# First layer's attention: one inverse of the softmax sums and a row of four scalings per four heads

## The chip, the cores and the metric

One core of a Trainium2 chip runs the whole program. The metric is the device time of one execution in microseconds (us). TensorE (PE) does matmuls, VectorE (DVE) and ScalarE (ACT) work on tiles of 128 partitions, GpSimd (POOL) does a few elementwise steps, and SyncE (SP) issues most DMA transfers. Each engine takes its instructions strictly in the order in which they stand in its queue.

## The reference

The program is a two-layer diffusion trunk over 512 latent and 256 context tokens of width 1024. The first layer mixes tokens in two ways at once: 8 heads of attention, and 8 heads of a linear recurrence that runs in both directions ("state mixing"). Their outputs are joined, multiplied by `w_out`, and an MLP follows. The part that the change touches is the softmax of the attention:

```python
s_lat = jnp.einsum('bqgrd,bkgd->bgrqk', q, kl) * scale      # latent keys
s_ctx = jnp.einsum('bqgrd,bkgd->bgrqk', q, kc) * scale      # context keys
p_lat, p_ctx = joint_softmax([s_lat, s_ctx])                # over both
o = einsum('bgrqk,bkgd->bqgrd', p_lat, vl) + einsum('bgrqk,bkgd->bqgrd', p_ctx, vc)
```

Context queries read the 256 context tokens only; latent queries read all 768 tokens.

## The kernel before

Attention and state mixing of the first layer share one stage. Tokens are cut into six tiles of 128; tiles 0 and 1 are context, 2 to 5 latent.

**Attention.** `attend` (lines 1126 to 1160) takes one tile of queries. Its 8 heads come as two groups of four (`g`), and a group shares keys and values. For each head `j` of a group: matmuls write the scores into `ps` (tag `sc`, two banks of PSUM, one buffer), DVE takes the row maximum (L1149) and makes the bias (L1151), ACT computes the exponentials into a tile `prob` with the row sum as a by-product (L1154), DVE inverts the sum (L1155), and ACT scales `prob` by it (L1156). `prob` has five buffers, so the second score of a group needs a buffer that the group before has to give back. Then `weighted` (lines 323 to 345) goes over the tiles of keys: four transposes (L332) put a 128x128 piece of each head into a bank `pt` (two buffers), ACT or DVE in turn copies it to `pts` (L337, L335), and a matmul adds values times weights to `po` (L341). Two such matmuls for neighbouring tiles use different halves of the array. At its end, ACT copies half of `po` and DVE adds the other half into `oa` (L344, L345), which ACT's queue stores to `oD` in DRAM (L1160). A group of a latent tile has 4 scores, 24 transposes, 6 copies and 6 value products; one of a context tile 4, 8, 2 and 2, on 256 keys.

**State mixing.** A chain of 24 steps. In a step: matmul `x` from the state (L1026), DVE add `xs`, matmul `u` (L1036), DVE `vu` (L1041, twice), matmul `s` (L1051), DVE `state` (L1059). Around the chain stand the preparation of the next block (`z`, `xv`, L985 to L1005) and the outputs (`y`, L1070 to L1080). When a pair of token tiles is complete, `finish` normalizes it: mean and variance on DVE and ACT, transposes `yt` (L1116), products `oy` (L1120, L1123), and a store to `oD` by POOL's queue (L1124). Loads `gg` for it stand in SP's queue (L1087, L1088) and wait for a buffer that L1123 gives back.

**What sets the order.** All functions are generators. The loop `state_mixing` moves them along: attention first gets 40 steps, then 5 per step of the chain, 120 in all. A step of the generator ends at each `yield`, so the place of a `yield` decides when its instructions are written down, and with that their priority; a scheduler then sorts each engine's queue by priority and by when it thinks the inputs are there. The chain has high priority, attention fills in. At the stage's end comes the product with `w_out` (L1302) for three segments: context (tiles 0, 1), the middle latent tiles (3, 4) and the outer ones (2, 5). It loads `raw` from `oD` (L1293), splits it into a high and a low part (`xr`, or `dh` and `dl`; L279 on ACT, L280 on DVE), and multiplies by weights which are split in the same way (`wraw`, `whi`, `wlo`). Its first PSUM bank is the one of the scores. One output tile of 256 columns takes 24 matmuls, and each segment has 8 such tiles.

Of the kernel before, what the change touches and what calls it, by code (L numbers as in the profile page):

```python
# [10 lines left out]
F32 = mybir.dt.float32  # L11
F32R = mybir.dt.float32r
AF = mybir.ActivationFunctionType
ALU = mybir.AluOpType
AX = mybir.AxisListType
# [3 lines left out]
P = 128  # L19
# [205 lines left out]
def tile_trunk(ctx: ExitStack, tc: tile.TileContext, t: dict, out, cc: Cols, pc: Cols):  # L225
    nc = tc.nc
    V, A, G, T = nc.vector, nc.scalar, nc.gpsimd, nc.tensor
# [7 lines left out]
    def u(s):  # L235
        uid[0] += 1
        return f"{s}_{uid[0]}"
# [648 lines left out]
    with ExitStack() as sb:  # L886
        psum_pool(sb, zy=(2, 1), ch=(1, 1), po=(1, 1), pt=(2, 1), sc=(1, 2))
        tp = pool("attention", stack=sb, side="right")
# [238 lines left out]
        def attend(qi, keys):  # L1127
# [9 lines left out]
            V.tensor_tensor(out=qs[64:128], in0=qr[64:128], in1=qs[64:128].bitcast(F32), op=ALU.subtract)  # L1137
            o = tp.tile([P, 512], F32, tag="oa", name=u("oa"), bufs=1)
            for g in (0, 1):
                prob = []  # L1140
                for j in range(4):
                    ps = psum("sc", "sc")
                    for s in SEGS:
                        if s[0] >= P * kt1:
                            continue
                        for m, kx in enumerate((kh, kl)):
                            T.matmul(ps[:, cols2(s)], lhsT=qs[:, 2 * j + g, :], rhs=kx[:, g, s[0]:s[0] + s[1]], start=m == 0, stop=m == 1)  # L1147
                    st = tp.tile([P, 4], F32, tag="st", name=u("st"), bufs=6)
                    V.tensor_reduce(out=st[:, 0:1], in_=ps[:, c0:c1], op=ALU.max, axis=AX.X)  # L1149
                    sc = sq8[:, qi, 2 * j + g:2 * j + g + 1]  # L1150
                    V.tensor_scalar(out=st[:, 1:2], in0=st[:, 0:1], scalar1=sc, scalar2=-1.0, op0=ALU.mult, op1=ALU.mult)  # L1151
                    pr = tp.tile([P, NT], F32, tag="prob", name=u("prob"), bufs=5)
                    pv = pr[:, 0:c1 - c0]
                    A.activation(out=pv, in_=ps[:, c0:c1], func=AF.Exp, scale=sc, bias=st[:, 1:2], accum_out=st[:, 2:3])  # L1154
                    V.reciprocal(out=st[:, 3:4], in_=st[:, 2:3])  # L1155
                    A.activation(out=pv, in_=pv, func=AF.Copy, scale=st[:, 3:4])  # L1156
                    prob.append(pr)
                    yield
                yield from weighted(prob, vtok, g, list(range(kt0, kt1)), o, tp)
            nc.scalar.dma_start(oD[0:4, :, P * qi:P * qi + P].rearrange("a q c -> q a c"), o.rearrange("p (a c) -> p a c", c=P))  # L1160

# [104 lines left out]
    with ExitStack() as sc:  # L1266
# [8 lines left out]
        scale = norm_scale(0, 4, "nmlp")  # L1275
# [528 lines left out]
```

## Time and profile before

| | us |
|---|---|
| median of 3 runs | 2008.81 (2007.28 to 2010.16) |
| the profiled execution: its own time | 2009.51 |
| its span, first to last instruction | 2007.7 |
| first `s` of the chain starts | 366.22 |
| last `s` of the chain starts | 612.20 |
| PE busy over the span | 1896.6 (94%) |
| DVE, ACT busy | 1215.2 (61%), 840.7 (42%) |

A busy PE is a modelled figure, because matmuls overlap: in a dense stretch, the distance from one start to the next says more than a duration. Times in the trace are counted from the first instruction.

### The profile page before, as it was taken

What the parts mean: (1) busy time and instruction counts of PE and PEld (TensorE: products, weight loads), DVE (VectorE), ACT (ScalarE), POOL (GpSimd) and SP (SyncE); (2) the same over time, 40 slices, a digit from 0 to 9 for tenths busy, and PEclk for the clock granted to TensorE, in tenths of its full rate; (3) what the DMA queues carried; (4) which work ended last, traced back from release to release, by engine and by line L of the source; (5) the groups of instructions that cost most, each with busy time, mean ns of one, the idle gap of its engine ahead of it and who ended that gap; (6) DMA issues with size and microseconds to landing.
All of it is one profiled execution on the core that took longest, in us unless ns stands there. A gap on an engine that the chain in (4) does not pass through costs nothing.

```text
span 2007.7 us, 34218 instructions
## 1 busy us (share of the span) xinstructions
PE 1896.6 (94%) x13992; PEld 1545.1 (77%) x13992; DVE 1215.2 (61%) x2150; ACT 840.7 (42%) x1419; POOL 294.2 (15%) x291
## 2 busy tenths in 40 slices
PE   6999988899998999999999999899899789999997
PEld 4776756776765998888888889778578488888886
DVE  5567979775677765654544444865687464444445
ACT  3344442555544552232223224544566454333335
POOL 0000014432321520000000002310153120000001
PEclk9999998899998999999999999999999799999998
DMA  9355575742414733344444422212101133333333
GB/s 336 121 166 171 182 228 148 156 89 56 98 44 132 251 107 99 122 124 136 125 125 121 136 84 80 76 53 74 32 1 53 32 95 105 95 92 97 95 97 113
DMA packets 147884, 228.18 MB, mean 114 GB/s; under 512 B 65024, under 2 KB 102288, under 8 KB 147600
## 3 DMA queue, kind: packets, MB, share of 16 engines
q1 hardware_dynamic: 140912, 213.54, 36.1%
q10 hardware_dynamic: 5456, 7.73, 1.1%
q0 software_dynamic: 1360, 4.73, 0.7%
q8 instruction: 110, 1.80, 0.4%
q14 instruction: 46, 0.38, 0.1%
HBM read 200.00 MB, written 25.96 MB: 113 GB/s over the span
## 4 chain that ended last, share of the span: by engine, by line
PE 77%; DVE 9%; DMA 7%; ACT 3%; issue 3%; POOL 1%; SPq 0%; DVEq 0%; POOLq 0%; ACTq 0%
PE m L367 37%; PE win L367 13%; PE po L341 4%; DMA wmod<-in_wmod_dram 4%; PE pt L332 3%; PE z L985 2%; DVE wlo L280 2%; PE sc L1147 2%; PE wout L1718 1%; PE wout L1302 1%; PE s L1051 1%; PE mod L405 1%; PE lora L653 1%; PE z L1560 1%; DVE junk L1319 1%
## 5 line engine op out<-in xcount | busy, mean ns | idle before, releaser
L279 ACT ACTIVATE whi<-wraw 128x1024 fp32r<-128x1024 f32 x214 | 226.4, 1059 | 678.0 <-PE m L367 561.0
L280 DVE TENSOR_TENSOR wlo<-wraw,whi 128x1024 fp32r<-128x1024 f32 x214 | 264.4, 1236 | 212.2 <-ACT whi L279 209.4
L367 PE MATMUL m<-hh,whi 128*128 128x512 f32 (+1 forms) x816 | 239.3, 344 | 4.9 <-ACT relu L1241 2.4
L367 PE MATMUL m<-hl,whi 128*128 128x512 f32 (+1 forms) x816 | 241.2, 343 | 0.2 <-POOL hl L503 0.2
L367 PE MATMUL m<-hh,wlo 128*128 128x512 f32 (+1 forms) x816 | 241.3, 344 | 0.0
L367 PE MATMUL m<-dl,whi 128*128 128x256 f32 (+1 forms) x832 | 240.7, 341 | 0.0
L367 PE MATMUL m<-dh,whi 128*128 128x256 f32 (+1 forms) x832 | 238.6, 342 | 1.7 <-DVE xl L1223 1.6
L367 PE MATMUL m<-dh,wlo 128*128 128x256 f32 (+1 forms) x832 | 239.8, 341 | 0.1
L367 PEld LDWEIGHTS m<-dh,whi 128*128 128x128 f32 x832 | 153.3, 188 | 23.9 <-DVE xl L1223 4.9
L367 PEld LDWEIGHTS m<-hh,whi 128*128 128x128 f32 x816 | 152.1, 188 | 24.7 <-ACT relu L1241 2.8
L471 POOL TENSOR_TENSOR acc<-acc,nsq 128x256 f32<-128x256 f32 x42 | 42.8, 1027 | 865.8 <-ACT nsq L470 861.0
L367 PEld LDWEIGHTS m<-hl,whi 128*128 128x128 f32 x816 | 153.6, 188 | 19.4 <-POOL hl L503 0.4
L367 PEld LDWEIGHTS m<-dl,whi 128*128 128x128 f32 x832 | 153.8, 188 | 19.0
L367 PEld LDWEIGHTS m<-dh,wlo 128*128 128x128 f32 x832 | 153.7, 188 | 18.9 <-DVE wlo L280 0.3
L367 PEld LDWEIGHTS m<-hh,wlo 128*128 128x128 f32 x816 | 153.4, 188 | 19.0 <-DVE wlo L280 0.3
L367 PE MATMUL win<-hl,whi 128*128 128x512 f32 (+1 forms) x512 | 162.3, 348 | 4.7 <-POOL hl L503 3.5
L367 PE MATMUL win<-hh,whi 128*128 128x512 f32 (+1 forms) x512 | 162.3, 362 | 2.7 <-ACT hh L498 2.7
L367 PE MATMUL win<-hh,wlo 128*128 128x512 f32 (+1 forms) x512 | 160.2, 345 | 0.0
L1319 DVE SCALAR_TENSOR_TENSOR junk<-wmod,crow 128x1024 f32<-128x1024 f32 x64 | 78.5, 1226 | 118.5 <-DMA wmod<-in_wmod_dram 117.9
L1223 DVE SCALAR_TENSOR_TENSOR xl<-m,modT,xl 128x512 f32<-128x512 f32 (+1 forms) x144 | 97.4, 686 | 72.3 <-PE m L367 72.3
L367 PEld LDWEIGHTS win<-hh,whi 128*128 128x128 f32 x512 | 95.4, 194 | 33.6 <-issue 15.7
L367 PEld LDWEIGHTS win<-hl,whi 128*128 128x128 f32 x512 | 98.5, 193 | 22.9 <-issue 5.7
(413 smaller groups left out, 3560.0 us busy)
## 6 DMA issues: line engine op xcount, KB each, us to landing
wraw<-in_w_dram SPq DMA_DIRECT2D x136, 512.0 KB, 3.6
wmod<-in_wmod_dram SPq DMA_DIRECT2D x96, 512.0 KB, 4.2
wraw<-in_wout_dram SPq DMA_DIRECT2D x40, 512.0 KB, 3.7
wraw<-in_win_dram SPq DMA_DIRECT2D x35, 512.0 KB, 4.4
arD<-ar SPq DMA_DIRECT2D x8, 768.0 KB, 4.5
kbD<-kb SPq DMA_DIRECT2D x8, 768.0 KB, 6.5
ari<-arD SPq DMA_DIRECT2D x24, 256.0 KB, 3.9
kbd<-kbD SPq DMA_DIRECT2D x48, 128.0 KB, 3.9
```

Source lines behind the costliest of these rows:

```text
L279: A.activation(out=hi, in_=src, func=AF.Copy)
L280: (lo_eng or V).tensor_tensor(out=lo, in0=src, in1=hi.bitcast(F32), op=ALU.subtract)
L332: T.transpose(pt[:, P * j:P * j + P], prob[j][:, P * m:P * m + P], ident)
L341: T.matmul(po[HALVES[i], :], lhsT=vt[:, k_, r], rhs=w_, start=m_ < 2, stop=m_ + 2 >= n, tile_position=(0, 64 * i))
L367: T.matmul(part(ps, s), lhsT=a[:, c], rhs=row(b, k, s), start=first and j == 0 and q == 0, stop=last and j == n - 1 and q == 2)
L405: T.matmul(ps[r:r + 32, :], lhsT=cs[:, k, :], rhs=wm[:, c], start=k == 0, stop=k == KT - 1, tile_position=(0, r))
L471: (V if k == KT - 1 else eng).tensor_tensor(out=at(acc, s), in0=at(acc, s), in1=at(sq, s), op=ALU.add)
L653: T.matmul(ps[s][d][:, 0:s[1]], lhsT=LORA[wname][r, P * p:P * p + P], rhs=src[r, tokens(s)], start=True, stop=True, tile_position=(64 * d, 0))
L985: T.matmul(ps[:, P * (2 * a + c):P * (2 * a + c) + P], lhsT=kb[:, 2 * m + a, c, :], rhs=ar[:, 2 * m + a, c, :], start=True, stop=True)
L1147: T.matmul(ps[:, cols2(s)], lhsT=qs[:, 2 * j + g, :], rhs=kx[:, g, s[0]:s[0] + s[1]], start=m == 0, stop=m == 1)
L1223: V.scalar_tensor_tensor(out=xs, in0=part(ps, s), scalar=mod(l, which, m, s[2]), in1=xs, op0=ALU.mult, op1=ALU.add)
L1319: V.scalar_tensor_tensor(out=junk, in0=wm, scalar=1.0, in1=crow[:, :, v], op0=ALU.mult, op1=ALU.mult, accum_out=modT[:, l, n, v:v + 1])
```

## The change

Per group of four heads, the four small tiles `st` (128x4, six buffers) become one tile of 128x4x4 (three buffers): a row of maxima, one of biases, one of sums and one of inverses. The loop over heads now ends with the exponentials. After it stand two more steps of the generator: an empty one, then one with a single `reciprocal` of four columns and the four scalings one after the other.

```diff
             for g in (0, 1):
-                prob = []
+                prob, st = [], tp.tile([P, 4, 4], F32, tag="st", name=u("st"), bufs=3)
                 for j in range(4):
                     ps = psum("sc", "sc")
...
-                    st = tp.tile([P, 4], F32, tag="st", name=u("st"), bufs=6)
-                    V.tensor_reduce(out=st[:, 0:1], in_=ps[:, c0:c1], op=ALU.max, axis=AX.X)
+                    V.tensor_reduce(out=st[:, 0, j:j + 1], in_=ps[:, c0:c1], op=ALU.max, axis=AX.X)
...
-                    A.activation(out=pv, in_=ps[:, c0:c1], func=AF.Exp, scale=sc, bias=st[:, 1:2], accum_out=st[:, 2:3])
-                    V.reciprocal(out=st[:, 3:4], in_=st[:, 2:3])
-                    A.activation(out=pv, in_=pv, func=AF.Copy, scale=st[:, 3:4])
+                    A.activation(out=pr[:, 0:c1 - c0], in_=ps[:, c0:c1], func=AF.Exp, scale=sc, bias=st[:, 1, j:j + 1], accum_out=st[:, 2, j:j + 1])
                     prob.append(pr)
                     yield
+                yield
+                V.reciprocal(out=st[:, 3], in_=st[:, 2])
+                for j in range(4):
+                    A.activation(out=prob[j][:, 0:c1 - c0], in_=prob[j][:, 0:c1 - c0], func=AF.Copy, scale=st[:, 3, j:j + 1])
+                yield
                 yield from weighted(prob, vtok, g, list(range(kt0, kt1)), o, tp)
```

Two more `yield`s in each of 12 groups make 128 steps of attention where there were 104. The 40 steps ahead of the chain and the 5 per step of it are as before. So the scheduler's order changes on every engine from the first step of the chain on. Counted in PE's queue ahead of the last `s` of the chain: of 48 scores 46 before, now 43; of 224 transposes 192, now 176; of 56 value products 46 (22 alone, 12 times two neighbours together), now 44 (18 alone, 13 times two). Behind it stand 2 scores, 32 transposes and 10 value products (all alone) before; now 5 scores, 48 transposes and 12 value products (10 alone, one pair). Up to the first `s` of the chain, PE's queue is the same.

The first place is PE's queue at the end of the stage, where the scores of the last group (`sc`) stand just ahead of the first product with `w_out` (`wout`). Before, the last rows ahead of it are these, with one score:

```order
L1070 MATMUL y_7041<-state_6986,ard_3282 64x64
L1072 MATMUL y_7041<-vu_7037,z_3286 64x64
L1072 MATMUL y_7041<-vu_7039,z_3287 64x64
L1116 MATMUL yt_7072<-cst,yacc 128x128 x4
L1147 MATMUL sc_5701<-kh,qs_5245 128x256
L1147 MATMUL sc_5701<-kl,qs_5245 128x256
L1147 MATMUL sc_5701<-kh,qs_5245 128x512
L1147 MATMUL sc_5701<-kl,qs_5245 128x512
L332 MATMUL pt_5725<-cst,prob_5688 128x128
L332 MATMUL pt_5743<-cst,prob_5688 128x128
L1302 MATMUL wout_7184<-xr,whi_7180 128x256 x2
```

Now two scores stand there, behind the value products of the group before:

```order
L341 MATMUL po_5869<-pts_5957,vtok 64x512
L1148 MATMUL sc_6091<-kh,qs_5642 128x256
L1148 MATMUL sc_6091<-kl,qs_5642 128x256
L1148 MATMUL sc_6091<-kh,qs_5642 128x512
L1148 MATMUL sc_6091<-kl,qs_5642 128x512
L341 MATMUL po_5869<-pts_6027,vtok 64x512
L1148 MATMUL sc_6111<-kh,qs_5642 128x256
L1148 MATMUL sc_6111<-kl,qs_5642 128x256
L1148 MATMUL sc_6111<-kh,qs_5642 128x512
L1148 MATMUL sc_6111<-kl,qs_5642 128x512
L1116 MATMUL yt_7027<-cst,yacc 128x128 x4
L1116 MATMUL yt_7038<-cst,yacc 128x128 x4
```

The first `wout` follows on the last row. From the last `s` of the chain to this point, PE's queue now holds five scores and all six value products of the group before, where it held two scores and four value products. Behind the first 24 `wout` matmuls, 24 transposes and 6 value products of the last group follow in both; before, they stood together, now 24 further `wout` matmuls stand among them.

The second place is DVE's queue between the bias of the last group's third score (`st_6052<-st_6052,sq_99`, L1151) and the split of the context rows (`xr`, L280), which the first `wout` reads. Before, from the maximum of the last score on:

```order
L1149 TENSOR_REDUCE st_5706<-sc_5701 128x1
L280 TENSOR_TENSOR wlo_7214<-wraw_7211,whi_7213 128x1024
L1123 TENSOR_TENSOR oy_7077<-oy_7077,gg_6472 128x512
L1100 TENSOR_SCALAR mean_7082<-mean_7082 128x8 x2
L1151 TENSOR_SCALAR st_5706<-st_5706,sq_99 128x1
L1101 TENSOR_TENSOR yacc<-yacc,mean_7082 128x512 x2
L1155 RECIPROCAL st_5706<-st_5706 128x1
L280 TENSOR_TENSOR xr<-raw_7165,xr 128x4x256 x2
```

Now:

```order
L1151 TENSOR_SCALAR st_6052<-st_6052,sq_99 128x1
L280 TENSOR_TENSOR dl_7097<-raw_7094,dh_7096 128x4x256
L1111 TENSOR_TENSOR yacc<-yacc,var_7011 128x512 x2
L1149 TENSOR_REDUCE st_6052<-sc_6111 128x1
L280 TENSOR_TENSOR wlo_7142<-wraw_7139,whi_7141 128x1024
L1120 TENSOR_TENSOR oy_7032<-yt_7027,gg_6857 128x256 x2
L1151 TENSOR_SCALAR st_6052<-st_6052,sq_99 128x1
L1120 TENSOR_TENSOR oy_7043<-yt_7038,gg_6860 128x256 x2
L1123 TENSOR_TENSOR oy_7032<-oy_7032,gg_6857 128x512
L1123 TENSOR_TENSOR oy_7043<-oy_7043,gg_6860 128x512
L1157 RECIPROCAL st_6052<-st_6052 128x4
L280 TENSOR_TENSOR xr<-raw_7093,xr 128x4x256 x2
```

Both splits of the middle tiles (`dl_7097`) and the end of `finish` for the last two tiles now stand ahead of the split of the context rows. ACT's queue has the same order: the exponentials of the last two scores, then `xr`, then the four scalings.

The third place is ACT's queue during the first `w_out` tiles, from the weights of the third tile (`whi_7176`) to those of the sixth (`whi_7281`); `dh_7098` is the outer segment, and its second row reads the attention rows that `L1162 DMA oD` stores:

```order
L279 ACTIVATE whi_7176<-wraw_7174 128x1024
L337 ACTIVATE pts_6228<-pt_6223 128x512
L467 ACTIVATE acc<-xc 128x256
L337 ACTIVATE pts_6264<-pt_6259 128x512
L279 ACTIVATE dh_7098<-raw 128x4x256
L337 ACTIVATE pts_6352<-pt_6347 128x512
L279 ACTIVATE whi_7211<-wraw_7209 128x1024
L344 ACTIVATE oa_5645<-po_6222 64x512
L1162 DMA oD<-oa_5645 128x4x128
L279 ACTIVATE whi_7246<-wraw_7244 128x1024
L279 ACTIVATE dh_7098<-raw 128x4x256
L279 ACTIVATE whi_7281<-wraw_7279 128x1024
```

Before, both rows of the outer segment stood together, one weight tile later: behind the weights of the sixth tile, ahead of those of the seventh. DVE's queue mirrors this with `dl_7099` ahead of `wlo_7282`.

More of the change, by code (lines that the diff above doesn't have):

```diff
@@ L1147, in attend @@
                             T.matmul(ps[:, cols2(s)], lhsT=qs[:, 2 * j + g, :], rhs=kx[:, g, s[0]:s[0] + s[1]], start=m == 0, stop=m == 1)
-                    st = tp.tile([P, 4], F32, tag="st", name=u("st"), bufs=6)
-                    V.tensor_reduce(out=st[:, 0:1], in_=ps[:, c0:c1], op=ALU.max, axis=AX.X)
+                    V.tensor_reduce(out=st[:, 0, j:j + 1], in_=ps[:, c0:c1], op=ALU.max, axis=AX.X)
                     sc = sq8[:, qi, 2 * j + g:2 * j + g + 1]
-                    V.tensor_scalar(out=st[:, 1:2], in0=st[:, 0:1], scalar1=sc, scalar2=-1.0, op0=ALU.mult, op1=ALU.mult)
+                    V.tensor_scalar(out=st[:, 1, j:j + 1], in0=st[:, 0, j:j + 1], scalar1=sc, scalar2=-1.0, op0=ALU.mult, op1=ALU.mult)
                     pr = tp.tile([P, NT], F32, tag="prob", name=u("prob"), bufs=5)
[L1153 to L1156, printed above, removed]
+                    A.activation(out=pr[:, 0:c1 - c0], in_=ps[:, c0:c1], func=AF.Exp, scale=sc, bias=st[:, 1, j:j + 1], accum_out=st[:, 2, j:j + 1])
                     prob.append(pr)
                     yield
+                yield
[3 more added lines that the diff above has]
+                yield
                 yield from weighted(prob, vtok, g, list(range(kt0, kt1)), o, tp)
```

## The prediction

> **What bounds the kernel now.** I read the page's chain first, then a table by stages, then the waits in the stage that the change touches.
>
> ```profile
> PE 77%; DVE 9%; DMA 7%; ACT 3%; issue 3%; POOL 1%; SPq 0%; DVEq 0%; POOLq 0%; ACTq 0%
> 366.00:613.00 247.00, 241.78 (x3620) 179.72 (x3620) 172.75 (x401) 137.00 (x271) 74.50 (x66) 0.98 0.37 80
> 613.00:633.00 20.00, 13.22 (x157) 7.66 (x153) 14.03 (x31) 7.60 (x12) 2.47 (x3) 0.88 0.42 132
> 633.00:648.00 15.00, 14.32 (x62) 8.66 (x61) 11.56 (x18) 7.30 (x10) 2.93 (x1) 0.82 0.64 211
> 648.00:718.00 70.00, 67.89 (x564) 66.38 (x563) 55.81 (x84) 40.16 (x65) 39.69 (x36) 1.00 0.72 229
> ```
>
> The columns of the last four are the stretch, its length, busy time (and instructions) of PE, PE's weight loads, DVE, ACT and POOL, the granted TensorE clock, the DMA share, and GB/s. The chain of the state runs from 366 to 613, and PE is idle there for 5.2 us of 247: this stretch is full. From 648 on, the product with `w_out` keeps PE full too (2.1 us idle in 70). Between them lie the weak spots: 6.8 us idle in 20, and a lower clock. So work that PE no longer does ahead of 613 shortens the first stretch; what it then does between 613 and 648, it does where PE waits for others.
>
> What the change attacks is seen in the waits of DVE and ACT in the same stretch, 366 to 613 (us in total, times, longest):
>
> ```profile
> DVE st L1155 <- ACT prob L1154: 8.7, 11, 1.5
> ACT prob L1156 <- DVE st L1155: 9.3, 16, 1.4
> ACT z L994 <- DVE st L1155: 7.8, 13, 0.9
> PE z L985 <- ACT z L994: 2.3, 1, 2.3
> ```
>
> DVE stands still in front of the inverse, ACT in front of the scaling. But PE hardly waits for either: the largest entry of PE's own list is the last row.
>
> **The change part by part.** Durations of the group's parts, from the groups of the same stretch (busy, mean ns of one, idle before):
>
> ```profile
> L1149 DVE TENSOR_REDUCE st<-sc 128x1 f32<-128x768 f32 x30 | 28.6, 954 | 9.3 <-PE sc L1147 9.1
> L1155 DVE RECIPROCAL st<-st 128x1 f32<-128x1 f32 x45 | 7.1, 158 | 9.0 <-ACT prob L1154 8.7
> L1154 ACT ACTIVATE prob<-sc,st,sq 128x768 f32<-128x768 f32 x29 | 28.7, 988 | 19.9 <-DVE st L1151 15.6 <-PE pt L332 2.2 <-PE x L1026 2.1
> L1154 ACT ACTIVATION_READ_ACCUMULATOR prob<-sc,st,sq 128x1 f32 x45 | 8.8, 195 | 0.0
> L1156 ACT ACTIVATE prob<-prob,st 128x768 f32<-128x768 f32 x29 | 27.0, 932 | 6.4 <-DVE st L1155 6.2
> ```
>
> *Inverses:* 12 in place of 48 saves 36 x 0.158 = 5.7 us of DVE, which is 30% idle there; worth nothing on the path by itself. An inverse of four columns isn't in this trace; between 0.16 (one column) and 1.0 us (a DVE pass over 768 columns, the row above it), I take 0.17, near the first. *The scalings* keep their 0.93 us each but now come as one block of 3.7 us in ACT's queue, behind the fourth exponential, and no transpose of a group can start before. The wait of a whole group for one inverse is new: queued behind it on DVE are the chain's `state` or `xs`, behind the block on ACT `z`, `xv` and the next exponential. Six groups of latent tiles are scaled ahead of the chain's end. At worst each holds PE by the block's excess over one scaling, 2.8 us, so 16.8; at best the waits listed above go and PE gets back its 5.2 idle us. Before, PE's queue passed over most such delays; I take nothing, nearer to the row of PE's waits.
>
> *Work moved past the end of the chain.* Prices from the timeline (start, us, instruction):
>
> ```profile
> 605.85 0.38 PE L1147 MATMUL sc<-kh,qs 128*128 128x256 f32 x1
> 606.75 0.91 PE L1002 MATMUL xv<-vm,zk 128*64 128x64 f32 x22
> 541.25 1.08 PE L341 MATMUL po<-pts,vtok 128*64 128x512 f32 x4
> 542.26 0.39 PE L1147 MATMUL sc<-kh,qs 128*128 128x256 f32 x1
> 639.08 1.07 PE L341 MATMUL po<-pts,vtok 128*64 128x512 f32 x2
> 640.09 0.66 PE L332 MATMUL pt<-cst,prob 128*128 128x128 f32 x4
> 640.68 1.07 PE L341 MATMUL po<-pts,vtok 128*64 128x512 f32 x2
> ```
>
> Start to start, a score takes 0.90, two neighbouring value products together 1.01 (two records each, x4), one alone 1.01 as well, four transposes 0.59. By the counts in the order, PE loses ahead of the last `s` 3 scores (2.7), 16 transposes (2.4), and in value products 34 slots less 31 (3.0): **-8.1 us**. The idle of the chain is taken as unchanged.
>
> *The end of the stage.* Let 0 be the end of the last `s`, 613.28 before:
>
> ```profile
> 613.28 1.07 PE L341 MATMUL po<-pts,vtok 128*64 128x512 f32 x2
> 632.71 0.58 PE L1302 MATMUL wout<-xr,whi 128*128 128x256 f32 x1 [5.55 <-ACT xr L279]
> 633.97 0.58 PE L1302 MATMUL wout<-xr,whi 128*128 128x256 f32 x1 [0.68 <-DVE xr L280]
> 634.34 0.41 PE L1302 MATMUL wout<-xr,wlo 128*128 128x256 f32 x1
> 634.98 0.41 PE L1302 MATMUL wout<-xr,wlo 128*128 128x256 f32 x1
> 638.52 0.28 PE L1302 MATMUL wout<-xr,wlo 128*128 128x256 f32 x1
> 638.87 0.28 PE L1302 MATMUL wout<-xr,wlo 128*128 128x256 f32 x1
> 648.48 0.50 PE L1302 MATMUL wout<-xr,whi 128*128 128x256 f32 x2
> 663.91 0.39 PE L1302 MATMUL wout<-xr,wlo 128*128 128x256 f32 x1 [0.80 <-DVE wlo L280]
> ```
>
> Before: `wout` runs from 20.7; the first tile is done at 25.8; six value blocks last to 35.2; then tiles of 8 x 0.35 = 2.8 us follow up to a stall that ends at 50.6, in the seventh tile.
>
> Now, by the new queues: the fourth score of the last group but one starts at 1.0, its maximum ends at 2.9, its exponential is read out at 5.7 (three `yacc`/`xs` passes of DVE lie between); the inverse at 6.5, behind `vu`; four scalings to 10.2; the next exponential (0.99 + 0.20) to 11.4, a copy `pts` to 12.0. Six blocks of 0.59 + 1.01 = 1.6 us start at 12.4, and the third score of the last group stands behind the fifth: 19.8 to 20.7. These rows price what follows:
>
> ```profile
> 638.26 0.17 DVE L381 TENSOR_SCALAR var<-var 128x16 f32<-128x16 f32 x1
> 646.16 0.75 DVE L1120 TENSOR_TENSOR oy<-yt,gg 128x256 f32<-128x256 f32 x2
> 649.20 0.69 DVE L345 TENSOR_TENSOR oa<-po,oa 64x512 f32<-64x512 f32 x1 [0.27 <-ACT oa L344]
> 654.31 1.06 ACT L279 ACTIVATE whi<-wraw 128x1024 fp32r<-128x1024 f32 x1 [1.41 <-PE wout L1302]
> 655.41 1.23 DVE L280 TENSOR_TENSOR wlo<-wraw,whi 128x1024 fp32r<-128x1024 f32 x1 [0.49 <-ACT whi L279]
> raw<-oD SPq DMA_DIRECT2D x4, 256.0 KB, 4.4
> oD<-oa ACTq DMA_DIRECT2D x1, 256.0 KB, 3.1
> ```
>
> DVE: maximum to 21.9, `var` 0.2, `dl` 1.2, `oa` 0.7, bias 0.2, 24.2 with the hand-overs; exponential to 25.5. The fourth score to 26.6; maximum, `wlo` 1.2, `oy` 0.8, bias: 30.0; exponential to 31.3. Only then ACT splits `xr` (32.4) and DVE its rest (33.7). So `wout` runs from 33.7, **13.0 us later** behind the last `s` than before.
>
> From there: the first tile to 38.7 (as before, at the lower clock); then 20 transposes (3.0), five slots of value products (5.0) and two tiles (5.6) to 52.3; that is better mixed than before. Two tiles more bring 58.0, and there the sixth waits: its weights stand behind the outer rows of the last attention tile. The last value product is some 2.6 us before 52.3; copy, addition and start of the store 1.3 (51.0), landing 3.1, load 4.4 with its issue 0.4 (58.9), split on ACT 1.1 and DVE 1.2, `wlo` 1.2: 62.4. Set on the same place (one tile more, 2.8): 65.2, against 50.6, **+14.6 us**.
>
> *Clock.* After the 5.55 us wait, three `wout` matmuls took 0.64 (634.34 to 634.98), later 0.35 (638.52 to 638.87), over about six threes: 1.8 us. The new end has a second wait, of some 3.7 us, ahead of the fourth score; I add 0.5, between 0 and 1.8. The Trainium skill, "TensorE: Matmul & The Clock Gate", section "Why this matters for your kernels", says that an idle gap of more than about 3 us puts TensorE back to half its clock. By that the second wait costs a full slow stretch and the sum is 1.3 us higher; the trace agrees with the rule for the 5.55 us gap.
>
> Sum: -8.1 + 14.6 + 0.5 = **+7.0 us**. Behind this place PE is full, so the shift stays to the end. Against the profiled execution's 2009.5 this is 2016.5; that execution lies 0.7 above the median shown, so the median comes to **2015.8**.
>
> **The rivals.** *A, faster: the removed hand-overs shorten the chain.* For it: 8.7 + 9.3 + 7.8 = 25.8 us of waits on DVE and ACT; PE's busy time is modelled, so idle can be hidden in it. If half came back, 12.9 us, the sum is -5.9: 2002.9. It decides from 7.0 us recovered on. Against it: PE's own list shows almost no wait for these engines.
>
> *B, no change: PE's work is conserved and the end catches up.* If the last two scores don't queue behind DVE's splits (2 x 2 us) and the last load lands before the sixth tile's weights are needed (about 3.5 us), the sum falls to -0.5: 2008. For it: the passes ahead of the biases are of low priority and might have been done earlier; against it: the order fixes them there.
>
> *C, slower still: the blocks of scalings hold up the chain.* Half of the 16.8 us gives +15.4: 2024. For it: `z` and `xv` stand behind such blocks, and PE once waited 2.3 us for `z`. Against it: they are prepared a block ahead. The Trainium skill, "Perfetto Trace Analysis", section "Optimizing Scalar/DVE Operations", says for engines that aren't saturated but cause bubbles on others: "breaking up instructions may allow work to be completed sooner." That speaks against this change, which does the reverse; ACT's 137 busy of 247 us shows an engine that isn't saturated. By the rule, it goes as in C.
>
> That the change doesn't do what it says is excluded by the order: 12 inverses, each ahead of four scalings.
>
> **How the numbers follow.** Forecast (slower by 3 to 11 us) 0.45, A 0.15, B 0.25, C 0.15. A measurement tells a difference from none at about 0.2%, 4 us. A is all faster; 0.03 of B and of the forecast's lower edge joins it, and 0.05 of the forecast lies within 4 us: faster 0.17, same 0.28, slower 0.55. Both signs are possible, so the range takes in A's value and C's: 2002.8 to 2025; the forecast alone has 2012 to 2020.
>
> **What would show it.** Right: the last `s` ends near 605; `wout` starts 33 us behind it, waiting for `xr` behind a last exponential; PE idles twice for 3 to 5 us in between, with a lower clock; a later stall of 4 us before the sixth `w_out` tile; from the seventh tile on, everything shifted by one amount. Wrong: an `s` chain that ends at 613 (C), or well ahead of 603 (A), or a first `wout` less than 27 us behind the last `s` (B). What I trust least is the idle of the chain: it was taken over unchanged, though every queue was sorted anew.

## The result, and the profile after

| | before | changed |
|---|---|---|
| median, us | 2009.49 (4 runs, 2007.28 to 2015.05) | 2023.32 (4 runs, 2021.57 to 2026.74) |
| ratio, 95% interval | | 1.0078 [1.0064, 1.0092] |
| profiled execution: its own time, its span | 2009.51, 2007.7 | 2022.97, 2021.2 |
| first `s`, last `s` start | 366.22, 612.20 | 363.12, 609.49 |
| from the first to the last `s` ("the chain") | 245.98 | 246.37 |
| end of the last `s` to where `wout` runs ("the end") | 20.6 | 32.1 |

Slower by 13.5 us between the two profiled executions, by about 16 by the ratio; a second timing on another chip (below) gave 1.0052, about 10 us. The forecast was +7.0, so the direction was right and the size about half.

The first view is the changed kernel's table by stages (stretch, length, busy time of PE, PE's weight loads, DVE, ACT, POOL, granted clock, DMA share, GB/s):

```profile
363.00:610.00 247.00, 234.45 (x3579) 175.81 (x3579) 165.68 (x358) 127.30 (x259) 74.80 (x66) 0.98 0.37 81
610.00:643.00 33.00, 22.26 (x202) 12.36 (x198) 26.60 (x52) 17.31 (x27) 7.55 (x6) 0.90 0.46 138
643.00:670.00 27.00, 25.27 (x157) 19.59 (x157) 12.11 (x15) 12.11 (x17) 0.91 (x2) 0.93 0.49 154
```

The first row of the table answers to the stretch 366 to 613 of before, which has the same length. PE is busy 234.45 us where it was 241.78: 7.3 us of work have left the chain, as forecast (8.1). But the chain isn't shorter: its idle went from 5.2 to 12.5 us, which is the same 7.3. In the second row PE stands idle for 10.7 of 33 us; before, that stretch of weakness was 6.8 of 20.

The waits in the chain's stretch, changed kernel (us in total, times, longest):

```profile
DVE st L1157 <- ACT prob L1153: 2.2, 4, 0.8
...
ACT prob L1159 <- DVE st L1157: 1.9, 3, 0.8
...
ACT z L994 <- DVE st L1157: 1.5, 1, 1.5
...
DVE xs L1029 <- ACT xv L1005: 6.3, 5, 3.1
...
PE sc L1148 <- ACT prob L1153: 3.2, 5, 2.3
...
PE y L1072 <- DVE vu L1041: 2.8, 4, 1.1
...
PE pt L332 <- ACT prob L1159: 1.4, 4, 0.4
```

What the change attacked is gone: the first three rows were 8.7, 9.3 and 7.8 us, 25.8 together, and are 5.6. PE got nothing of it. In its own list scores now wait for exponentials (3.2, before 1.0), and transposes for scalings (before: no such row). One wait of the chain itself grew: DVE's `xs` for `xv`, 6.3 us in five waits, where it was 1.3 in two.

The end, from the timeline of the changed kernel (start, us, instruction, wait):

```profile
609.49 1.15 PE L1051 MATMUL s<-vu,z 64*64 64x64 f32 x32 [0.15 <-DVE st L1151]
...
634.28 0.39 PE L1148 MATMUL sc<-kh,qs 128*128 128x256 f32 x1 [3.14 <-ACT prob L1153]
...
641.48 0.58 PE L1304 MATMUL wout<-xr,whi 128*128 128x256 f32 x1 [3.79 <-ACT xr L279]
...
642.74 0.58 PE L1304 MATMUL wout<-xr,whi 128*128 128x256 f32 x1 [0.68 <-DVE xr L280]
...
670.40 0.38 PE L1304 MATMUL wout<-xr,wlo 128*128 128x256 f32 x1 [0.95 <-DVE wlo L280]
```

From the end of the last `s` (610.64 with its 1.15) it is 23.6 us to the last score, with a wait of 3.14 for the exponential ahead of it, 32.1 to where `wout` runs (its second product, behind another wait of 3.79 and the short stall of 0.68), and 59.8 to the end of the stall ahead of the sixth `w_out` tile. These are the places that the forecast named.

### The profile page after: what moved, and what is told of

It reads as the page before. It is cut to its first block, busy times and chain, and to the rows that moved or that the text cites. A ratio compares the mean times of both kernels' runs of the same rounds, so it can differ in the third digit from the quotient of the medians.

```text
span 2021.2 us, 34210 instructions
## 1 busy us (share of the span) xinstructions
PE 1900.2 (94%) x13992; PEld 1547.7 (77%) x13992; DVE 1209.1 (60%) x2114; ACT 838.2 (41%) x1419; POOL 294.5 (15%) x291
## 4 chain that ended last, share of the span: by engine, by line
PE 61%; DVE 9%; DMA 5%; ACT 3%; issue 3%; POOL 1%; DVEq 0%; POOLq 0%; ACTq 0%; SPq 0%
PE m L367 37%; PE win L367 4%; PE po L341 3%; DMA wmod<-in_wmod_dram 3%; PE pt L332 2%; PE wout L1304 2%; PE z L985 2%; DVE wlo L280 2%; PE wout L1720 1%; PE sc L1148 1%; PE z L1562 1%; DVE junk L1321 1%; PE s L1051 1%; PE y L1072 1%; DVE st L1149 1%
## 5 line engine op out<-in xcount | busy, mean ns | idle before, releaser
L280 DVE TENSOR_TENSOR wlo<-wraw,whi 128x1024 fp32r<-128x1024 f32 x214 | 263.8, 1234 | 215.7 <-ACT whi L279 213.0
L367 PEld LDWEIGHTS win<-hl,whi 128*128 128x128 f32 x512 | 98.9, 194 | 22.9 <-issue 5.7
```

The costliest lines, as they stand in the source:

```text
L280: (lo_eng or V).tensor_tensor(out=lo, in0=src, in1=hi.bitcast(F32), op=ALU.subtract)
L367: T.matmul(part(ps, s), lhsT=a[:, c], rhs=row(b, k, s), start=first and j == 0 and q == 0, stop=last and j == n - 1 and q == 2)
```

## The experiments

Three numbers serve all of them: PE's idle in the chain (length of the stretch less PE's busy time), the end as defined above (counted from behind the short stall that follows `wout`'s first product or two), and the **gap** of a group: from the end of the sum of its last exponential to the first copy of its transposes (`pts<-pt`), read from the timeline and added up over the eight latent groups (before 29.5 us, changed 46.0, so 3.7 and 5.8 a group).

Some rivals fall without a run, by the compiled order. The changed kernel without its two added `yield`s gives the same order on PE, DVE, ACT and POOL, row for row; so does before with two empty `yield`s added; and four single inverses moved behind the loop over the heads, each ahead of its scaling, give the order of before. Neither the pace of the generator nor the place in the code changes these queues, and the two added `yield`s aren't what sorted them anew: what acts is that one inverse reads four sums.

**Pairs.** One inverse for two scores, behind the second:

```diff
+                    if j % 2:
+                        V.reciprocal(out=st[:, 3, j - 1:j + 1], in_=st[:, 2, j - 1:j + 1])
+                        for i in (j - 1, j):
+                            A.activation(out=prob[i][:, 0:c1 - c0], in_=prob[i][:, 0:c1 - c0], func=AF.Copy, scale=st[:, 3, i:i + 1])
```

> One inverse for two scores, with its two scalings right behind the second exponential. Measures: chain = start of the first `s` to start of the last (before 246.0 us, changed 246.4); end = from the end of the last `s` to where `wout` runs (20.7 and 32.2). Priced as in the prediction, PE's queue holds 228.0 us of work in the chain (before 223.8, changed 215.8; the rest of the chain was 22.2 and 30.6 us of idle), and the scores behind the last `s` are again those of before. Theory H (a block of scalings on ACT holds `xv`, `z` and the exponentials, in proportion to its excess over one scaling): idle 22.2 + 8.4/3 = 25.0, chain 253, end about 21, time about 2016. Rival S (the idle comes from the new order itself, uneven steps with a floor of latency, not from the block): idle 30.6, chain 258.6, time about 2022. Theory T alone (only the end costs, no block costs anything): chain 250.2, time about 2013.5.

Measured: 1.0025 [1.001, 1.0041], about +5 us; chain 246.4, idle 6.4, end 19.2, gap 34.1. The end is that of before, as all theories had it; the chain is shorter than each of them allowed (250 to 259), so the priced work was too high: priced, pairs hold 4.2 us more in the chain than before (228.0 and 223.8), but PE is busy there for 0.8 us less (240.0 and 240.8). The idles of 22 to 31 us in the expectations of the first three runs rest on such prices; from here on, idle is read from PE's busy time.

**Preparation first.** Does the block on ACT hold `xv` and `z`?

```diff
-                        advance(todo)
+                        with tc.high_priority():
+                            advance(todo)
```

> The changed kernel, with the preparation of the next block (`ari`, `z`, `xv`) put ahead of the attention on every queue. The blocks of four scalings stay as they are. PE's queue holds 216.8 us in the chain (changed: 215.8), and one score fewer stands behind the last `s` than in the changed kernel. H: `xv` and `z` no longer stand behind a block, the idle goes back to about 22, chain 239, end 29 to 32, time 2012 to 2015. S: idle 30.6 as in the changed kernel, chain 247.4, time 2020 to 2024.

Measured: 1.0103 [1.0081, 1.0124], +21; chain 252.0, idle 10.2, end 29.1, gap 49.2. Theory H gave 2012 to 2015 and is missed by far. By the trace the edit did half of what it was for. Add up for how long, within the chain, ACT runs scalings while a finished `xv` product still waits to be copied: 1.8 us before, 9.6 in the changed kernel, 2.4 here. For `z` it is 0.7, 6.4 and 7.5. So `xv` is mostly out of the block's reach, `z` isn't, and the kernel is slower still.

**Scalings in halves.**

```diff
-                    A.activation(out=prob[j][:, 0:c1 - c0], in_=prob[j][:, 0:c1 - c0], func=AF.Copy, scale=st[:, 3, j:j + 1])
+                    for h in (prob[j][:, 0:(c1 - c0) // 2], prob[j][:, (c1 - c0) // 2:c1 - c0]):
+                        A.activation(out=h, in_=h, func=AF.Copy, scale=st[:, 3, j:j + 1])
```

> The changed kernel, with each scaling split into two halves of the columns (eight short ones behind one inverse). Broken-up work can let others in between; each piece also pays its own start, so ACT's sum grows. PE's queue holds 223.0 us in the chain, and two scores fewer stand behind the last `s` than in the changed kernel. H, with the pieces letting `xv` and `z` through: idle 22, chain 245, end 26 to 29, time 2016 to 2019. S, or pieces that don't let anything through: idle 30.6, chain 253.6, time 2024 to 2028.

Measured: 1.0158 [1.0133, 1.0183], +32: worse than both theories. Idle 17.8, chain 264.2, gap 47.1. The block isn't opened, it is longer (eight pieces in 4.14 us, four full ones in 3.41). The Trainium skill, "Perfetto Trace Analysis", section "Optimizing Scalar/DVE Operations", has it that breaking up may let work complete sooner; cutting the scalings by columns didn't do so here.

**The floor of a step.** The attention of the four latent tiles is left out of the kernel before:

> The kernel before without the attention of the last four of the six tiles (their rows are filled by a copy). It leaves the chain alone on PE from about its sixth step on: 15 steps with 5.5 to 6.5 us of PE work each (mean 5.9). It measures the floor of one step, which no attention fills. S: a floor of 8.5 us or more, so a step with less work than that is idle anyhow, and the 15 steps take 128 us or more. H: a floor at or below the shortest step of the changed kernel (7.2 us), so the 15 steps take 105 to 112 us, and a step of 8 us or more isn't bound by it.

Measured: 1932.53 us (one run); the last 15 steps take 109.4 us, the shortest 5.7. So no floor of latency lies under the light steps of 7 to 9 us; rival S falls.

**Thin scalings**, in the changed kernel and, as a control, in the kernel before: only one column of every 128 is scaled.

```diff
+                    pv = prob[j].rearrange("p (m x) -> p m x", x=P)[:, 0:kt1 - kt0, 0]
+                    A.activation(out=pv, in_=pv, func=AF.Copy, scale=st[:, 3, j:j + 1])
```

> The changed kernel with each scaling cut to one column of every 128 (the probabilities of the other columns stay unscaled): one inverse for four scores and every dependency stay, the block shrinks from four times 0.85 us to four short instructions. By the new order, two scores stand behind the last `s` as in the kernel before (changed: five). PE's idle in the chain, from the profile: 5.2 us before, 12.5 changed, 17.8 with eight half scalings. H (the block's length on ACT holds the chain and puts scores behind it): idle 5 to 7, end 19 to 22, time 2003 to 2011. Rival G (the wait of a whole group for one inverse does it, however short the scalings): idle 11 or more, end 25 or more, time 2016 or more.

> The control to the thin scalings: the kernel before with the same cut of each scaling to one column of every 128 and one inverse per score. No score stands behind the last `s` in its order. H: ACT's relief alone brings little, since the chain is full of PE's work; idle 4 to 6, time 2003 to 2009, and the thin changed kernel differs from it by less than 6 us (against 15.7 with full scalings). G: the thin changed kernel stays 12 us or more behind it.

Measured: thin changed 1.0042 [1.0031, 1.0054], idle 9.9, gap 39.3; thin before 1.0023 [1.0013, 1.0033], idle 4.3, gap 20.6. A block of four now lasts 0.89 us, less than a single full scaling (0.93), and yet idle and gap stay well above the control's. The time is G's by the first expectation, the end (17.8) is still below H's, the idle lies between. But against the control, on the same chip, the loss is only 4.4 us between the medians: less than H's 6 and far from G's 12, where the full block costs 10 to 16. So the length of the block carries much of the loss (it is also how long the transposes behind it wait), and it is not all of it.

**All scalings on DVE**, batched and, as a control, each behind its own inverse (`V.tensor_scalar(out=pv, in0=pv, scalar1=..., scalar2=None, op0=ALU.mult)` in place of the `A.activation`):

> The changed kernel with all four scalings on DVE instead of ACT, still one block behind one inverse. By the order five scores stand behind the last `s`, as in the changed kernel. H in the narrow form (it is ACT's queue, with `xv`, `z` and the exponentials, that the block holds): idle 5 to 8, end about 30, time 2014 to 2019. H in the wide form (a block holds whatever stands behind it, and on DVE that is the chain's own `xs`, `vu` and `state`): idle 12 or more, time 2024 to 2034.

> Control to the block of four on DVE (25.7 us over before): the kernel before with each scaling on DVE right behind its own inverse. PE holds 223.9 us in the chain (221.1 there) and four scores behind the last `s` (five there). H: the single scaling holds DVE's `xs`, `vu` and `state` by no more than its own length; 10 us or more faster than the twin, time 2010 to 2024. R: as slow, time 2028 to 2038.

Measured: batched 1.0132 [1.0118, 1.0145], idle 14.3, end 40.0; single 1.0106 [1.0087, 1.0126], idle 14.4, end 27.0. Taken alone that is the wide form of H, but by the pair it is R's case: the batch costs some 4 to 5 us, the two intervals overlap, and work put on DVE, the chain's own engine, costs either way.

**The copy `xv` on DVE**, in the kernel before:

> The kernel before with the copy `xv` on DVE instead of ACT, nothing else. By the order no score stands behind the last `s` (two before), so some 2 us of PE work go into the chain and the end is shorter by a score and its wait. H: `xv` is out of reach of ACT's queue, idle 3 to 5, end 14 to 19, time 2002 to 2008. Rival: DVE's queue holds `xv` as ACT's did and the chain grows by what it takes in; time 2008 to 2014.

Measured: 1.0084 [1.0068, 1.01], +17; idle 10.7, chain 256.6. Missed by both theories; it says the same of work put on DVE. Whether ACT's queue holds the chain in the changed kernel it can't tell, since it swaps one queue for another.

**Controls without the batch** to the second and third run: before with the preparation first, and before with the scalings in halves.

> Control to the changed kernel with the preparation first (21 us over before): the kernel before, one inverse per score, with the preparation of the next block put ahead of the attention in the same way. By its order PE holds about the same work in the chain (216.4 us priced, 216.8 there) and the same four scores behind the last `s`. H (batching of the scalings holds the chain, under any order): 8 us or more faster than its batched twin, time 2005 to 2019. Rival R (the loss is that of a re-sorted order: any disturbance puts other long passes, such as the splits of `qs` and `wraw` and the passes of the group norm, in front of the chain's inputs; batching is only one way to disturb): as slow as its twin, time 2022 to 2032.

> Control to the eight half scalings (32.6 us over before): the kernel before with each scaling in two halves right behind its own inverse, so blocks of two short ones. PE holds 221.3 us in the chain and three scores behind the last `s` (223.0 and three there). H: the longer sum of the scalings costs only where it comes in one block; 15 us or more faster than the twin, time 2009 to 2024. R: as slow as the twin, time 2030 to 2042.

Measured: 1.0048 [1.0029, 1.0067] and 1.0044 [1.003, 1.0059]; idle 6.0 and 7.4, gaps 27.1 and 27.7. Each disturbed order loses 9 us even without a batch (R has a part), but each batched twin loses 11 and 23 us more, and in all five pairs (full, thin, halves, preparation first, DVE) the batched one is slower, though for DVE not beyond the intervals, and its gap is longer by 15 to 22 us. So what is it that the batch holds?

**Three and one, one and three.** The inverse is cut in two, behind the loop:

```diff
-                V.reciprocal(out=st[:, 3], in_=st[:, 2])
+                V.reciprocal(out=st[:, 3, 0:3], in_=st[:, 2, 0:3])
+                V.reciprocal(out=st[:, 3, 3:4], in_=st[:, 2, 3:4])
```

and in the other kernel `0:1` and `1:4`.

> The changed kernel with the inverse of four cut into one of the first three scores, ready an exponential earlier, and one of the last, both behind the fourth score's row. By the order two scores stand behind the last `s` as before (five in the changed kernel), and PE holds 227.9 us in the chain. H: three scalings can run before the last exponential's sum is there, the block is nearly that of four and the idle stays above 8 us, but the end is that of before: time 2010 to 2018. R: an order like any other: time 2015 to 2030.

> The cut the other way round: one inverse of the first score, one of the other three, both behind the fourth score's row. ACT gets blocks of three as in the cut three-and-one, but now the three stand behind the last exponential (some 2.6 us of scaling ahead of the first transpose; 0.9 in three-and-one and in the kernel before, 1.7 in pairs, 3.4 in the changed kernel). By the order three scores stand behind the last `s`, PE holds 220.1 us in the chain. Theory L (what counts is the scaling between a group's last exponential and its first transpose): between pairs (+5 us) and the changed kernel (+15.7), time 2015 to 2022, idle in the chain 8 to 12. Theory H (the length of the block on ACT): as three-and-one, time 2002 to 2010, idle near 5. Theory R (any order by chance): no relation, 2005 to 2030.

> The changed kernel itself, on the chip of the cut kernels beside it: 15 us over before, 2021 to 2026, as measured earlier; L, H and R expect the same.

> Three-and-one once more, beside the changed kernel and one-and-three. If its gain over before (3.4 us between the medians, ratio 0.9978) is real, the ratio comes out between 0.996 and 0.9995 again, and it is 17 to 21 us faster than the changed kernel; if it was the scatter of one chip, the ratio lies around 1.000 or above. L and H both expect the gain; R says nothing.

Measured: three-and-one 0.9978 [0.9964, 0.9991], again 0.9979 [0.9966, 0.9992]: about 4 us **faster than before**, where H and R had both expected a loss at first; 15 us faster than the changed kernel beside it, where 17 to 21 were expected. One-and-three 1.005 [1.0031, 1.0068], a time as L had it (its idle, 13.0, is above L's 8 to 12), and as slow as the changed kernel beside it, 1.0052 [1.0033, 1.0072] (2020.15 us, a little under what was expected). The chain's stretch of three-and-one (second timing), then of one-and-three, in the columns of the stage table:

```profile
367.00:612.00 245.00, 240.37 (x3641) 179.41 (x3640) 168.60 (x379) 136.10 (x272) 73.77 (x66) 1.00 0.34 80
```

```profile
361.00:612.00 251.00, 238.03 (x3605) 176.72 (x3605) 168.53 (x374) 132.09 (x266) 74.04 (x66) 0.98 0.35 79
```

Idle 4.6 and 13.0, with blocks of three in both: the length of a block alone falls as the cause. L stands, but not as the sum of the scalings in between, since thin scalings sum to less than one full one. What differs shows in one group's exponentials, scalings and transposes. Before (its last exponential is the one at 550.77):

```profile
543.07 0.38 PE L332 MATMUL pt<-cst,prob 128*128 128x128 f32 x2
...
544.46 0.44 PE L332 MATMUL pt<-cst,prob 128*128 128x128 f32 x2
...
550.26 0.44 PE L332 MATMUL pt<-cst,prob 128*128 128x128 f32 x2
...
550.77 0.98 ACT L1154 ACTIVATE prob<-sc,st,sq 128x768 f32<-128x768 f32 x1
...
552.65 0.94 ACT L1156 ACTIVATE prob<-prob,st 128x768 f32<-128x768 f32 x1 [0.80 <-DVE st L1155]
...
554.79 0.44 PE L332 MATMUL pt<-cst,prob 128*128 128x128 f32 x2
...
555.19 0.59 ACT L337 ACTIVATE pts<-pt 128x512 f32<-128x512 f32 x1
```

The same group of the changed kernel:

```profile
557.20 0.99 ACT L1153 ACTIVATE prob<-sc,st,sq 128x768 f32<-128x768 f32 x1 [2.54 <-PE z L985]
...
558.54 3.41 ACT L1159 ACTIVATE prob<-prob,st 128x768 f32<-128x768 f32 x4
...
559.11 0.39 PE L1148 MATMUL sc<-kh,qs 128*128 128x256 f32 x1
...
562.09 0.87 PE L332 MATMUL pt<-cst,prob 128*128 128x128 f32 x6
...
563.69 0.38 PE L332 MATMUL pt<-cst,prob 128*128 128x128 f32 x2
...
564.00 0.60 ACT L337 ACTIVATE pts<-pt 128x512 f32<-128x512 f32 x1 [0.38 <-PE pt L332]
```

The transposes of two key tiles (two `pt` buffers, four heads each: eight) can be under way at a time. Before, PE did them head by head between the scores, six of the eight ahead of the last exponential; only the last head's two were left. Behind one inverse of four all eight stand behind the last exponential and the block, and behind the first score of the next group (559.11). By the compiled orders and what the transposes read, this count of those that don't wait for the last exponential is six in before, three-and-one and all kernels with single inverses, four in pairs, two in one-and-three, none with one inverse of four. The traces have these counts in every one of the eight latent groups (three-and-one in six of them, four and five in the other two).

**The transposes alone.** The inverse of four and a block of four scalings stay; the scalings of a latent group cover only 512 of 768 columns, in one kernel the last, in its twin the first, the others stay unscaled:

```diff
-                    A.activation(out=prob[j][:, 0:c1 - c0], in_=prob[j][:, 0:c1 - c0], func=AF.Copy, scale=st[:, 3, j:j + 1])
+                    pv = prob[j][:, 0:c1 - c0] if qi < 2 else prob[j][:, 2 * P:c1 - c0]
+                    A.activation(out=pv, in_=pv, func=AF.Copy, scale=st[:, 3, j:j + 1])
```

> The changed kernel, where the four scalings of a latent group leave out the first 256 of the 768 columns (those probabilities stay unscaled). The transposes of the group's first two key tiles, the two that the transposes' buffers hold, then don't wait for the inverse of four; in PE's queue they stand behind each head's own exponential, six of eight or more ahead of the group's last one, as in the kernel before. The inverse of four and a block of four scalings of 512 columns stay. Theory T (the batch costs because the transposes that PE used to do ahead of the last exponential now wait for it): no more loss, no score behind the last `s`, idle 4 to 7, time 2000 to 2010. Theory H (the block on ACT, or the wait for one inverse of four, as such): as its twin with the first 512 columns scaled, slower than before by 6 us or more.

> The twin: the four scalings of a latent group leave out the last 256 of the 768 columns instead. Block and inverse are as long as there, but the transposes of the first two key tiles wait for them, none of the eight ahead of the group's last exponential, as in the changed kernel. By the order three scores stand behind the last `s`. T: slow like the changed kernel, time 2014 to 2024, idle 9 or more, at least 8 us behind its twin. H: equal to its twin within 4 us.

Measured: with the first two key tiles free 1.0003 [0.9991, 1.0014], with them held 1.0074 [1.006, 1.0088]; 14 us apart on the same inverses and blocks of the same length (711 and 713 ns a scaling). The two stretches, free and held:

```profile
367.00:625.00 258.00, 248.40 (x3678) 183.35 (x3677) 171.59 (x374) 130.97 (x275) 74.13 (x66) 0.99 0.33 76
```

```profile
363.00:619.00 256.00, 240.14 (x3597) 179.14 (x3598) 168.72 (x361) 125.40 (x265) 75.86 (x66) 0.98 0.35 78
```

Free: 248.40 us of work in 258, idle 9.6 (T had 4 to 7), no score behind the last `s`, end 17.5, gap 8.2. Held: 8.3 us less work in a chain of nearly the same length, idle 15.9, three scores behind, end 25.9, gap 39.3. The only edit between the twins is which columns are scaled, so which transposes wait; the orders differ as well, because the scheduler sorts by that. What the batch costs hangs on the transposes that wait for it.

How these 14 us come about is shown less well than that they do. The twins differ in one thing more: a finished `xv` product waits while ACT runs scalings for 8.6 us in held, for 1.6 in free (8.6 in one-and-three, 1.6 in three-and-one). If that were what holds PE, PE's `u`, which needs `xs` and so `xv`, would wait longer in held. It doesn't; free, then held:

```profile
PE sc L1148 <- ACT prob L1153: 2.9, 3, 1.8
...
PE u L1036 <- DVE xs L1029: 2.2, 3, 1.5
```

```profile
PE sc L1148 <- ACT prob L1153: 5.5, 7, 2.3
...
PE po L341 <- DVE pts L335: 2.2, 1, 2.2
...
PE u L1036 <- DVE xs L1029: 1.5, 4, 0.7
```

What grows in held is PE's idle ahead of the attention's own scores and value products, which fits a PE that runs out of other work. With the preparation first, `xv` was mostly out of reach (2.4 us, its control 1.8), and the batch still cost 11 us. So `xv` behind the block is at most a part. And the kernels with six of eight ahead that put no work on DVE lie anywhere from -4 to +10 us, so 14 us is the price in this pair, not a constant.

All kernels in one table; "ahead" is that count of eight, "behind" the scores that the compiled order has behind the last `s`:

| kernel | ahead | behind | idle | gap | end | ratio |
|---|---|---|---|---|---|---|
| before | 6 | 2 | 5.2 | 29.5 | 20.6 | 1 |
| three and one (second timing) | 6 | 2 | 4.6 | 29.4 | 16.8 | 0.9979 |
| free | 6 | 0 | 9.6 | 8.2 | 17.5 | 1.0003 |
| pairs | 4 | 2 | 6.4 | 34.1 | 19.2 | 1.0025 |
| one and three | 2 | 3 | 13.0 | 41.3 | 27.5 | 1.0050 |
| changed | 0 | 5 | 12.5 | 46.0 | 32.1 | 1.0078, 1.0052 |
| held | 0 | 3 | 15.9 | 39.3 | 25.9 | 1.0074 |
| thin, changed / before | 0 / 6 | 2 / 0 | 9.9 / 4.3 | 39.3 / 20.6 | 17.8 / 21.0 | 1.0042 / 1.0023 |
| preparation first | 0 / 6 | 4 / 4 | 10.2 / 6.0 | 49.2 / 27.1 | 29.1 / 26.0 | 1.0103 / 1.0048 |
| halves | 0 / 6 | 3 / 3 | 17.8 / 7.4 | 47.1 / 27.7 | 29.9 / 24.1 | 1.0158 / 1.0044 |
| DVE | 0 / 6 | 5 / 4 | 14.3 / 14.4 | 40.2 / 25.4 | 40.0 / 27.0 | 1.0132 / 1.0106 |
| `xv` on DVE (before) | 6 | 0 | 10.7 | 22.9 | 20.8 | 1.0084 |

## Why the prediction was half right

**The step that failed: "The idle of the chain is taken as unchanged."** The sum took -8.1 us from the chain for work that leaves it. The work left (7.3 us of busy time), the chain stayed as long (+0.4), and the idle took the room: 12.5 us for 5.2. The text's own sign of being wrong came up: counted from the same first `s`, the last one ends at 613.7 (610.64 and the 3.1 by which the execution was ahead), where it had put C at 613 and itself near 605. The term of the sum was 0 for the scalings ("I take nothing"), by the row of PE's waits, in which nothing waited for scalings. That row showed the order of before, where PE had other work, the transposes of three heads, between the exponentials; the change took just that cover away. The text had the fact in hand ("no transpose of a group can start before") and priced it by the block's length on ACT (3.7 us, measured 3.41), not by the transposes that PE would lose as filler. It also named the idle of the chain as what it trusted least.

**Rival C was right in size, not in its reason.** Half of its 16.8 is 8.4 us, and the chain lost 8.5 against the forecast. That its time, 2024, lies next to the measured 2023.3 is in part luck: its end was 2.6 us too large, 3.9 us came further on, and the second timing gave +10. And "`z` and `xv` stand behind such blocks" holds up `xs` visibly in one step, around 480; the other four times that `xs` waits for `xv`, an exponential stands ahead on ACT:

```profile
479.05 3.40 ACT L1159 ACTIVATE prob<-prob,st 128x768 f32<-128x768 f32 x4
...
481.68 0.44 PE L332 MATMUL pt<-cst,prob 128*128 128x128 f32 x2 [0.39 <-ACT prob L1159]
...
482.35 0.36 ACT L1005 ACTIVATE xv<-xv 128x256 f32<-128x256 f32 x1
...
482.75 0.42 DVE L1029 TENSOR_TENSOR xs<-x,xv 128x256 f32<-128x256 f32 x1 [3.09 <-ACT xv L1005]
```

ACT's block ends, `xv` follows, DVE's `xs` of the chain has waited 3.09 us; PE meanwhile does transposes at the pace of the scalings. Taking `xv` mostly out of the block's reach didn't help, and cutting the block by columns made it worse; holding or freeing the transposes decides.

**The end was right in mechanism, 2.6 us too large.** First `wout` at 32.1 against 33.7; the waits of 3.14 and 3.79 us stand where they were forecast, on an exponential and on `xr` behind the last one; the stall ahead of the sixth tile ends at 59.8 against 62.4, set on the same place (2.8 more) 62.6 against 50.6 before: +12.0 for +14.6. The extra 0.5 for the clock wasn't there: both traces have one stretch of 10.24 us at a clock of 0.50 (628.15 to 638.39 before, 636.33 to 646.57 now). The text's "the trace agrees with the rule for the 5.55 us gap" reads too much into before: there the clock fell 1.0 us into that gap (last section).

**The price of the inverse was right**: 0.17 us taken, 173 ns measured. A slip in the chances (0.15 and 0.03 make 0.18, not 0.17) changes nothing.

**Rival A fell.** The hand-overs did go (25.8 to 5.6 us of waits on DVE and ACT), and PE recovered nothing.

**"The shift stays to the end" was nearly right.** The MLP starts 9.6 us later than before (727.83 against 718.27): -3.1 that both executions differ by ahead of the first `s`, where PE's queue is the same, +0.4, +12.0 and 0.3 left over. The span ends 13.5 later; the 3.9 us between came in small pieces further on, and nothing was tried on them. One executed profile isn't worth that much: three-and-one had profiled executions of 2008.42 and 2001.98 us.

Why three-and-one beats before isn't shown as sharply. Its chain was 1.3 and 2.2 us shorter, its end 3.6 and 3.9; its order also differs from that of before, and before with the preparation first shows that a new order alone can move the time by 10 us.

## What to carry to other kernels

Before joining small operations into one, list what consumes their results one at a time: an engine that shows no wait for them may be filling its time with just these consumers, and a join makes all of them wait for the last. Count these in the queues (here six of eight transposes), and price them as lost filler on the bounding engine, not by the length of the joined block alone. Where the last part is what arrives late, join the others and leave it alone: here three and one kept the consumers ahead and was 4 us faster than before.

## What the runs showed of the hardware that was not expected

Cutting a scaling on ACT saves little: 768 columns took 929 ns, 384 took 603, 128 took 389, 6 took 295. From the chain of halves and of thin:

```profile
L1160 ACT ACTIVATE prob<-prob,st 128x384 f32<-128x384 f32 x51 | 26.5, 603 | 0.8 <-DVE st L1157 0.8
```

```profile
L1160 ACT ACTIVATE prob<-prob,st 128x6 f32<-128x6 f32 x28 | 6.2, 295 | 1.1 <-DVE st L1157 1.1
```

On DVE the mean of one scaling of 768 columns from SBUF, 862 ns, mixes two cases. The mean of the chain, then a block of four alone, then one beside POOL's work:

```profile
L1160 DVE TENSOR_SCALAR prob<-prob,st 128x768 f32<-128x768 f32 x24 | 19.2, 862 | 0.1
```

```profile
481.03 2.21 DVE L1160 TENSOR_SCALAR prob<-prob,st 128x768 f32<-128x768 f32 x4
```

```profile
453.36 2.36 POOL L976 TENSOR_TENSOR ard<-ari,dsel 64x512 f32<-64x512 f32 x2 [2.90 <-PE y L1070]
453.78 4.99 DVE L1160 TENSOR_SCALAR prob<-prob,st 128x768 f32<-128x768 f32 x4
455.80 1.24 POOL L1017 TENSOR_TENSOR old<-state,dds 128x512 f32<-128x512 f32 x1
```

In the first block each takes 0.62 us, a third less than on ACT; in the second 1.04 to 1.40. In the chains of both DVE kernels every scaling of 768 columns above 0.7 us (up to 1.90) overlaps POOL's L976 or L1017; not every overlap made one long, and no run was made without POOL's work.

The clock around a gap of PE. The changed kernel around its wait of 3.14 us (631.14 to 634.28), before around its wait of 5.55 (from 627.15), the kernel with the preparation first around one of 2.70 (637.13 to 639.83); the clock is in the third column from the end:

```profile
631.00:634.00 3.00, 0.14 (x1) 0.00 (x0) 3.00 (x6) 2.39 (x3) 2.58 (x1) 1.00 0.00 0
634.00:636.00 2.00, 1.00 (x5) 0.56 (x5) 1.02 (x3) 0.23 (x2) 1.19 (x1) 1.00 0.00 0
636.50:637.50 1.00, 1.00 (x6) 0.72 (x4) 1.00 (x3) 0.00 (x0) 0.00 (x0) 0.50 0.00 0
```

```profile
626.00:628.00 2.00, 0.44 (x2) 0.20 (x2) 2.00 (x5) 0.66 (x1) 0.00 (x0) 1.00 0.89 274
629.00:632.00 3.00, 0.00 (x0) 0.00 (x0) 2.90 (x8) 1.37 (x3) 0.75 (x1) 0.50 1.09 355
```

```profile
637.00:640.00 3.00, 0.30 (x2) 0.17 (x2) 2.20 (x6) 1.90 (x4) 0.00 (x0) 0.99 1.06 353
640.00:642.00 2.00, 1.39 (x4) 0.67 (x4) 1.25 (x2) 0.79 (x2) 0.00 (x0) 0.50 0.92 291
```

Each time the clock went to half, but not at the same distance: by the traces' records of the clock 2.05 us behind the end of the first gap, with PE at work and still ahead of the wait of 3.79 us; 1.0 us into the second; 0.12 us behind the third. So the length of one gap, and the prediction's limit of about 3 us, doesn't tell when the clock falls. In all the traces the slow stretches, except the last of each, are whole multiples of 3.41 us (3.41, 6.83, 10.24 and so on). The Trainium skill, "TensorE: Matmul & The Clock Gate", section "What's actually happening", describes a window of 3413 ns in which activity is watched and which runs freely; these lengths agree with it. That the moment of the fall depends on where a gap lies in this window would fit the three falls, and they don't show it.
